# A hybrid attention and recurrence layer: the output-product units of one query tile put into other steps, and one unit moved forward from a later tile

## The chip, the cores and the metric

The kernel runs on one core of a Trainium2 chip. The metric is device time in microseconds, the median of the runs. The core has a matrix engine (PE, with its weight loads shown apart as PEld), a vector engine (DVE), a scalar engine (ACT), a general engine (POOL, also called GpSimd) and a queue engine (SP) that only issues transfers. Each works through its own instructions in the order in which the program wrote them, and waits at an instruction until what it needs is there.

## The reference

One encoder layer over 16 meta tokens and 1024 positions of width 1024:

```
u = rms_norm(h);  q, k, v, g_att, x_lru, g_lru = split(u @ w_in)
p1, p2 = softmax(q1 k1), softmax(q2 k2)      # four heads, two maps a head, chunk-causal
o = rms_norm((p1 - lam * p2) @ v) * silu(g_att)
y = rg_lru(conv(x_lru)) * silu(g_lru)        # a linear recurrence over the positions
h = h + concat(o, y) @ w_out;  return rms_norm(h)[meta tokens left out]
```

## The kernel before

The first part is the input projections, the recurrence and the gates. The rest, from about 245 us of the span, is the attention with the two output products; the change touches it. It works on eight tiles of 128 query rows, in the order 3, 7, 6, 5, 4, 2, 1, 0. Each tile has four **steps**, one for each head, so steps 4 to 7 are tile 7, steps 8 to 11 tile 6, 12 to 15 tile 5, 16 to 19 tile 4, 20 to 23 tile 2, 24 to 27 tile 1 and 28 to 31 tile 0. A tile sees only the keys up to its own end: its score rows are 784 wide in tile 5, 656 in tile 4, 400 in tile 2 and 272 in tile 1. Below, "(5,1,0)" is the first of the two maps of head 1 of tile 5.

A step runs work of four heads at different stages, in this order of writing (function `attend`):

- `transposes` of the head three steps back: PE turns the weights `w` into `pt`, and ACT copies `pt` to `wT`; for tiles 4 and up in two halves, one here and one later in the step;
- `scores`, first map: PE forms `pss`; DVE reads it with the mask, takes the extreme value `mx` and writes `e` (the custom instruction); ACT takes the exponential of `e` and its sum;
- **output-product units**, as many as one third of the step's number in the table `MF` asks for, rounded;
- `combine` of the head one step back: on DVE a reciprocal, a small product and one pass (`SCALAR_TENSOR_TENSOR`) that joins the two maps into `e`;
- units up to two thirds, then the second half of the transposes, `scores` of the second map, and the rest of the units;
- `halve`: DVE splits the joined weights into two 16-bit halves (`CAST` and `TENSOR_TENSOR`, both to `w`); POOL copies the first 16 columns (`wm`);
- `weighted` of the head four steps back: PE multiplies `wT` with the values into the bank `O`.

In the first steps the table places pieces of the value projection. From step 7 on a **unit** is half of an output product for 512 columns: six matmuls, `psol` for the recurrence part and `psoa` for the attention part. After each second unit the vector engine adds the bank to a row tile (`xres` or `res`). The units wait in a list `fill` and are taken in a fixed order; the table `MF` says only how many are written in which step. So the table decides what stands between two pieces of attention on PE, and, by the additions, on DVE.

When a tile's four heads are weighted, `finish` takes over, and its pieces are written between the units and steps as a planner's clock finds them due (`pace`, called after each unit, each `scores` and each `weighted`). The pieces: ACT copies the bank `O` to `o` and squares it head by head (`sq`, four instructions); DVE scales the sums (`sums`); POOL takes the power (`sums`, `pw`), multiplies (`rec`), and makes two passes over `o` (with `gate`, then with `rec`); PE transposes `o` into the bank `pa`; ACT copies it (`af`); POOL splits it into `at` (`CAST`, `TENSOR_TENSOR`). Tile 7 finishes in steps 12 to 14, tile 6 in 16 to 18, tile 5 in 20 to 23, tile 4 in 24 to 27.

Three PSUM banks serve `pt`, `ptm` (the transposed meta columns), `pa` and, up to step 19, `psol`; a bank taken by a `psol` whose two units stand in different steps is held over the steps between. Two double banks serve `pss`; from step 20 they are cut up: two single banks for `pss` and two for `psol` and `psoa`. Score rows therefore need the vector engine to have read the row two before. The recurrence part is loaded by POOL (`lr`) when the product before it starts.

Every engine instruction of this part goes through one helper, so the line shown is L77 throughout; groups are told apart by the names of their tiles.

Of the kernel before, what the change touches and what calls it, by code (L numbers as in the profile page):

```python
# [98 lines left out]
def hybrid_layer_kernel(ctx: ExitStack, tc: tile.TileContext, xT, x, meta, w6, nwT,  # L99
# [684 lines left out]
    def load_q(i):  # L784
        q = slot("work", [P, 2, NMAP, P], F16, name="qt")
        c = slice(i * P, (i + 1) * P)
        d = qk_d[G_Q]
        dma(q[:, 0], d[:, :, c].rearrange("m p t -> p m t"))
        dma(q[0:64, 1], d[:, 64:128, c].rearrange("m p t -> p m t"))
        dma(q[64:128, 1], d[:, 0:64, c].rearrange("m p t -> p m t"))  # L790
        QT[i] = q
# [112 lines left out]
    def combine(i, h):  # L904

        d = st[i]
        n = d["n"]
        e0, e1 = d["e"][h, 0], d["e"][h, 1]
        V.reciprocal(d["rec"][:, :, h], d["sm"][:, :, h])
        rat = d["mx"][:, 1, h:h + 1]  # L910
        V.tensor_scalar(rat, d["rec"][:, 1, h:h + 1], nlam, d["sm"][:, 0, h:h + 1], op0=OP.mult, op1=OP.mult)
        V.scalar_tensor_tensor(e0[:, 0:n], e1[:, 0:n], rat, e0[:, 0:n], op0=OP.mult, op1=OP.add)
        w = d["w"][h] = slot("work", [P, 2, T], F16, name="w16")
        if i in PH:
            A.copy(w[:, 0, 0:n], e0[:, 0:n])
# [218 lines left out]
    def pace():  # L1134
        if paced[0] is None:
            paced[0] = clock.now["PE"]
        while clock.now["PE"] - paced[0] >= CH:
            paced[0] += CH
            tick(CH)
# [11 lines left out]

    filled = [0]

    MF = [8, 5, 10, 5, 2, 5, 5, 4, 1, 3, 3, 0, 1, 1, 0, 2, 1, 2, 3, 0, 1, 2, 2, 0, 2, 3, 1, 2, 1, 3, 1, 3, 2, 3, 0, 0]

    def at_least(n):
        while fill and filled[0] < n:
            fill_one()
# [35 lines left out]
    def attend():  # L1194
# [4 lines left out]
        def trans(hl):  # L1199
            if tra:  # L1200
                i, h = tra
                if i < 4 and hl == 1:
                    return
                transposes(i, h, hl)
                pace()

        for s in range(NS + TL + 1):
# [10 lines left out]
            if cur:  # L1218
# [4 lines left out]
                if h == QH and i in after:  # L1223
                    load_q(after[i])
            at_least((MF[s] + 2) // 3)
            if com:
                combine(*com)
            at_least((2 * MF[s] + 2) // 3)
            trans(1)
            if cur:  # L1230
                scores(i, h, 1)
                pace()
            at_least(MF[s])
            if com:
# [101 lines left out]
```

## Time and profile before

| what | value |
|---|---|
| runs shown | 484.71, 485.53 and 485.62 us |
| median | 485.53 us |
| the profiled execution's own time | 484.72 us |
| its span, first to last instruction | 482.9 us |
| around the span | 1.8 us |
| granted TensorE clock, mean | 0.997 |

The busy shares of the span are 96% for PE, 76% for DVE, 63% for ACT and 26% for POOL. A row of the timeline gives the start, the length, the engine, the line, the operation with the tiles written and read, the shape and the count, and in brackets the idle time of that engine just before and what ended it. Consecutive instructions of one kind are one row, and the length of a matmul row includes its drain, so rows of PE overlap: distances of starts tell more than lengths. The chain of waits follows the end of the program back to what released each piece.

### The profile page before, as it was taken

Reading aid. Unit: us, or ns where it says so; the run is one execution under the profiler, and the core shown is the slowest. Engines: PE = TensorE matmul, PEld = TensorE weight load, DVE = VectorE, ACT = ScalarE, POOL = GpSimd, SP = SyncE. Lnnn points to the kernel's source line nnn. Section 1 sums busy time; section 2 is a strip of 40 time slices with the busy share of each in tenths; the row PEclk is TensorE's granted clock in tenths of the full one; section 3 lists DMA queues with packets and bytes.
Section 4 is the critical chain, followed back from the end, with each engine's and each line's share of the span. In section 5 each row is a group of like instructions: output and inputs, shape, how many; then the busy total and the mean of one; then the engine's idle time right before and its main releaser. Section 6 shows DMA issues by size and latency. Waiting matters only on the chain.

```text
span 482.9 us, 7747 instructions
## 1 busy us (share of the span) xinstructions
PE 464.7 (96%) x2844; PEld 375.5 (78%) x2844; DVE 365.6 (76%) x612; ACT 302.9 (63%) x591; POOL 125.8 (26%) x171
## 2 busy tenths in 40 slices
PE   6999999999999999999999999999988999999894
PEld 5998989988888888888876677777766778877783
DVE  5768987496798676974574476889999989898443
ACT  5788333673627838432583467698787877797633
POOL 0104102201110000000101054185142425365772
PEclk9999999999999999999999999999999999999998
DMA  7994321253022115249454134965943475405523
GB/s 225 385 393 163 103 73 46 66 154 88 23 69 85 44 43 175 87 149 331 135 163 163 45 77 141 257 166 101 263 111 99 132 186 153 126 28 198 195 88 131
DMA packets 50150, 68.33 MB, mean 141 GB/s; under 512 B 21008, under 2 KB 30128, under 8 KB 50112
## 3 DMA queue, kind: packets, MB, share of 16 engines
q1 hardware_dynamic: 38096, 55.00, 34.7%
q0 software_dynamic: 11872, 12.63, 11.4%
q8 instruction: 22, 0.36, 0.3%
q10 hardware_dynamic: 144, 0.20, 0.1%
q14 instruction: 16, 0.13, 0.1%
HBM read 48.91 MB, written 18.91 MB: 140 GB/s over the span
## 4 chain that ended last, share of the span: by engine, by line
PE 81%; DVE 10%; issue 3%; ACT 3%; DMA 1%; POOL 0%; POOLq 0%; DVEq 0%; ACTq 0%; SPq 0%
PE pss L77 39%; PE psv L77 9%; PE psol L77 7%; PE psoa L77 7%; PE psx L77 5%; PE O L77 4%; PE ps L77 3%; DVE e L77 3%; PE psg L77 2%; PE pt L77 2%; DVE w L77 2%; DVE sp L77 2%; DVE XL L77 1%; DVE xc L77 1%; PE psmr L77 1%
## 5 line engine op out<-in xcount | busy, mean ns | idle before, releaser
L77 PE MATMUL pss<-xs,w 128*128 128x512 f32 (+1 forms) x720 | 142.4, 345 | 4.2 <-ACT xs L77 4.2
L77 PEld LDWEIGHTS pss<-xs,w 128*128 128x128 f32 x720 | 120.4, 190 | 24.5 <-ACT xs L77 4.2
L77 ACT ACTIVATE e<-e,mx 128x528 f32<-128x528 f32 (+7 forms) x64 | 50.5, 789 | 27.4 <-DVE mx L77 26.1
L77 PE MATMUL psv<-w,xs 128*128 128x512 f32 x192 | 48.4, 403 | 0.2 <-DVE v L77 0.2
L77 DVE CUSTOM_DVE_ANT_0 e<-pss,mask,nesc 128x528 f32<-128x528 f32 (+6 forms) x56 | 42.6, 761 | 7.7 <-PE pss L77 6.5
L77 PE MATMUL pss<-w,xs 128*128 128x512 f32 x192 | 46.0, 394 | 0.0
L77 PE MATMUL psol<-woh,lr 128*128 128x512 f32 x128 | 42.8, 415 | 2.0 <-ACT wT L77 2.0
L77 DVE TENSOR_TENSOR w<-wraw,w 128x512 fp32r<-128x512 f32 (+2 forms) x49 | 31.7, 669 | 15.4 <-ACT w L77 15.3
L77 PE MATMUL pss<-kst,qt 128*128 128x512 f16 (+3 forms) x208 | 42.6, 318 | 0.7 <-DVE mx L77 0.7
L77 PEld LDWEIGHTS psv<-w,xs 128*128 128x128 f32 x192 | 35.3, 188 | 10.0 <-issue 0.8
L77 PEld LDWEIGHTS pss<-w,xs 128*128 128x128 f32 x192 | 35.7, 188 | 7.9
L77 PE MATMUL psoa<-woh,at 128*128 128x512 f32 (+1 forms) x136 | 41.6, 389 | 0.2 <-ACT psoa L77 0.2
L77 ACT COPY wT<-pt 128x1024 f16<-128x1024 f16 (+5 forms) x48 | 37.6, 784 | 1.0 <-PE pt L77 0.8
L77 DVE SCALAR_TENSOR_TENSOR e<-e,mx 128x528 f32<-128x528 f32 (+7 forms) x32 | 35.0, 1093 | 1.1
L77 ACT ACTIVATE w<-wraw 128x512 fp32r<-128x512 f32 x47 | 28.6, 621 | 10.4 <-DMA wraw<-in_w_dram 9.9
L77 PE MATMUL ps<-xs,w 128*128 128x512 f32 x120 | 34.4, 394 | 0.0
L77 PEld LDWEIGHTS <-wT 128*128 128x128 f16 x432 | 25.6, 98 | 6.6 <-issue 2.7
L77 PE MATMUL O<-v,wT 128*128 128x128 f16 x432 | 29.4, 219 | 1.3 <-ACT wT L77 1.3
L77 DVE TENSOR_TENSOR w<-e,w 128x528 f16<-128x528 f32 (+7 forms) x32 | 28.9, 904 | 0.9
L77 PEld LDWEIGHTS psol<-woh,lr 128*128 128x128 f32 x128 | 22.9, 188 | 8.6 <-ACT wT L77 3.2
L77 DVE RECIPROCAL a<-a 128x208 f32<-128x208 f32 x20 | 27.8, 1423 | 0.0
L77 PEld LDWEIGHTS psoa<-woh,at 128*128 128x128 f32 x136 | 24.1, 188 | 4.6 <-ACT psoa L77 0.4
(200 smaller groups left out, 838.3 us busy)
## 6 DMA issues: line engine op xcount, KB each, us to landing
wraw<-in_w_dram SPq DMA_DIRECT2D x47, 256.0 KB, 4.2
xt<-in_x_dram SPq DMA_DIRECT2D x8, 512.0 KB, 6.8
woraw<-in_w_out_dram SPq DMA_DIRECT2D x8, 512.0 KB, 3.5
xres<-in_x_dram SPq DMA_DIRECT2D x8, 512.0 KB, 4.6
lr<-lru_d POOLq DMA_DIRECT2D x8, 512.0 KB, 5.3
res_d<-xres SPq DMA_DIRECT2D x8, 512.0 KB, 3.2
res<-res_d SPq DMA_DIRECT2D x8, 512.0 KB, 4.4
out_dram<-res SPq DMA_DIRECT2D x7, 512.0 KB, 2.9
```

Of the source, the lines that this page charges most:

```text
L77: return f(*a, **k)
```

## The change

Five numbers of the table `MF` are changed. In steps 12 to 15 (tile 5) the units are 0, 2, 2, 1 where they were 1, 1, 0, 2: five in place of four. In step 21, the second step of tile 2, there is one in place of two. The sum over all steps is the same.

```
-    MF = [8, 5, 10, 5, 2, 5, 5, 4, 1, 3, 3, 0, 1, 1, 0, 2, 1, 2, 3, 0, 1, 2, 2, 0, 2, 3, 1, 2, 1, 3, 1, 3, 2, 3, 0, 0]
+    MF = [8, 5, 10, 5, 2, 5, 5, 4, 1, 3, 3, 0, 0, 2, 2, 1, 1, 2, 3, 0, 1, 1, 2, 0, 2, 3, 1, 2, 1, 3, 1, 3, 2, 3, 0, 0]
```

The instructions are the same, none is added or removed. Between step 14 and step 20 the program is one unit further on in the list than before, from step 21 on it is level again. The planner's clock also moves pieces of `finish`.

PE around the end of step 13 and step 14, before; `pa` is the transposed output of tile 7, `w_3324` the weights of head 3 of tile 6:

```order
L77 LDWEIGHTS wT
L77 MATMUL O<-v,wT 128x128
L77 MATMUL pa<-idf,o 128x128 x4
L77 LDWEIGHTS w_3324
L77 MATMUL pt<-idh,w_3324 128x128
```

and now, in step 14:

```order
L77 MATMUL pss<-kst,qt 128x272
L77 MATMUL psol<-woh,lr 128x512 x2
L77 MATMUL psol<-wol,lr 128x512
L77 MATMUL psol<-woh,lr 128x512 x2
L77 MATMUL psol<-wol,lr 128x512
L77 MATMUL pa<-idf,o 128x128 x4
L77 MATMUL psol<-woh,lr 128x512 x2
```

The transposition of tile 7's output stood directly behind step 13; it now has the first transposes and scores of step 14 and one unit ahead of it.

DVE in step 13, before; `sums_2521` are the sums of squares of tile 7:

```order
L77 ISA mx_3288 128x1
L77 TENSOR_SCALAR sums_2521<-sums_2521 128x4
L77 CAST w_3324<-e 128x912
L77 TENSOR_TENSOR w_3324<-e,w_3324 128x912
L77 ISA e,mx_3288<-pss,mask,nesc 128x784
L77 ISA mx_3288 128x1
L77 TENSOR_TENSOR xres<-xres,psol 128x512
```

and now:

```order
L77 ISA mx_3288 128x1
L77 CAST w_3307<-e 128x912
L77 TENSOR_TENSOR w_3307<-e,w_3307 128x912
L77 TENSOR_SCALAR sums_2521<-sums_2521 128x4
L77 ISA e,mx_3288<-pss,mask,nesc 128x784
L77 ISA mx_3288 128x1
```

The scaling of the sums has changed places with the two instructions that split the weights of head 3 of tile 6 (the number behind `w` is only that of the buffer).

DVE in steps 16 and 17, before; `sums_2918` are the sums of squares of tile 6, the 656-wide rows are the scores of tile 4:

```order
L77 RECIPROCAL rec_3289<-sums_3287 128x2
L77 TENSOR_SCALAR mx_3288<-rec_3289,nlam,sums_3287 128x1
L77 SCALAR_TENSOR_TENSOR e<-e,mx_3288 128x784
L77 ISA e,mx_3615<-pss,mask,nesc 128x656
L77 ISA mx_3615 128x1
L77 CAST w_3651<-e 128x784
L77 TENSOR_TENSOR w_3651<-e,w_3651 128x784
L77 TENSOR_SCALAR sums_2918<-sums_2918 128x4
```

and now:

```order
L77 TENSOR_TENSOR xres<-xres,psol 128x512
L77 RECIPROCAL rec_3289<-sums_3287 128x2
L77 TENSOR_SCALAR mx_3288<-rec_3289,nlam,sums_3287 128x1
L77 SCALAR_TENSOR_TENSOR e<-e,mx_3288 128x784
L77 TENSOR_SCALAR sums_2918<-sums_2918 128x4
L77 ISA e,mx_3627<-pss,mask,nesc 128x656
L77 ISA mx_3627 128x1
L77 CAST w_3658<-e 128x784
```

Here the scaling of the sums has moved forward, ahead of a row of scores and of the split, and an addition of a finished `psol` stands ahead of the reciprocal.

## The prediction

> **What bounds the kernel now.** I read the page's busy shares first, then the busy time by stretches of the span, then the chain of waits, then the timelines of PE and DVE from step 12 on.
>
> ```profile
> span 482.9 us, 7747 instructions
> PE 464.7 (96%) x2844; PEld 375.5 (78%) x2844; DVE 365.6 (76%) x612; ACT 302.9 (63%) x591; POOL 125.8 (26%) x171
> ...
> 363.00:378.00 15.00, 13.69 (x123) 10.18 (x120) 14.68 (x28) 12.39 (x29) 3.15 (x5) 1.00 0.56 141
> ...
> 393.00:409.00 16.00, 15.41 (x143) 12.68 (x143) 15.59 (x34) 13.45 (x36) 7.17 (x10) 1.00 0.61 149
> 409.00:425.00 16.00, 16.00 (x117) 12.93 (x116) 13.65 (x46) 12.34 (x37) 5.93 (x10) 1.00 0.39 116
> ```
>
> Over the whole span PE is the bound (96%), but the shares hide two stages. The columns of a stretch are its length, then PE, PEld, DVE, ACT and POOL. From 363 to 378 (tile 5 into tile 4) DVE is busy for 14.68 of 15.00 us and PE for 13.69. From 393 to 409 (tile 2) both are nearly full. From 409 on PE is full and DVE has room. The granted clock is 1.00 in all three. So DVE sets the pace in tile 5, the two run level in tile 2, and after that PE does. The chain says the same:
>
> ```profile
> 356.52 1.03 DVE e L77
> ...
> 371.12 0.94 DVE e L77
> ...
> 397.55 2.79 PE psol L77 x12
> ```
>
> It lies on DVE from 356.52 to 371.12 and on PE in tile 2. Where DVE leads, PE waits:
>
> ```profile
> 355.56 0.55 PE L77 MATMUL pt<-idh,w 128*128 128x128 f16 x7 [0.69 <-ACT wT L77]
> ...
> 359.43 0.66 PE L77 MATMUL pa<-idf,o 128*128 128x128 f32 x4 [1.49 <-POOL o L77]
> ...
> 365.89 0.73 PE L77 MATMUL psol<-woh,lr 128*128 128x512 f32 x2 [1.08 <-ACT wT L77]
> ...
> 378.39 0.73 PE L77 MATMUL psol<-woh,lr 128*128 128x512 f32 x2 [0.30 <-ACT wT L77]
> ...
> 393.59 0.50 PE L77 MATMUL pss<-kst,qt 128*128 128x400 f16 x2 [0.67 <-DVE mx L77]
> ```
>
> That is 3.56 us before tile 2 and 0.67 at its first scores. There both PE and DVE meet: the banks of `pss` are cut up at that point, so PE may not go on before DVE has read the last row of tile 4. This wait makes the sum simple. Up to it only the time at which DVE arrives counts, and PE's work ahead of it is free as long as it fits into the 4.23 us of waits. Behind it PE has the work that is left.
>
> **The change part by part.** *The unit.* The chain's row gives 2.79 us for twelve matmuls, so a unit of six is 1.40 us of PE. One more stands ahead of the meeting point, one fewer behind it. If DVE arrives at the same time and never holds PE up afterwards, the program ends 1.40 us earlier: **−1.40**. PE's waits have room for it, 4.23 against 1.40. The addition to `xres` after each second unit moves along, but both orders have five of them ahead of tile 2's first row of scores; the sixth follows it at once now, and one step later before.
>
> *DVE up to the meeting point.* It has four gaps or coming gaps:
>
> ```profile
> 354.75 0.17 DVE L77 TENSOR_SCALAR sums<-sums 128x4 f32<-128x4 f32 x1 [0.85 <-ACT sq L77]
> ...
> 387.06 0.90 DVE L77 CUSTOM_DVE_ANT_0 e<-pss,mask,nesc 128x656 f32<-128x656 f32 x1 [0.55 <-PE pss L77]
> ...
> 388.49 0.69 DVE L77 TENSOR_TENSOR xres<-xres,psol 128x512 f32<-128x512 f32 x1 [0.52 <-PE psol L77]
> ...
> 416.14 0.17 DVE L77 TENSOR_SCALAR sums<-sums 128x4 f32<-128x4 f32 x1 [1.89 <-ACT sq L77]
> ```
>
> The first goes: the scaling of tile 7's sums now stands behind a `CAST` and a `TENSOR_TENSOR`. ACT's squares also start one `wT` copy later, so I look at whether the cover is enough:
>
> ```profile
> 354.62 0.88 ACT L77 COPY wT<-pt 128x896 f16<-128x896 f16 x1
> 355.41 0.95 ACT L77 ACTIVATE e<-e,mx 128x784 f32<-128x784 f32 x1
> ```
>
> A copy takes 0.79 from start to start, so the squares end at about 355.5. DVE is free 0.85 ahead of 354.75, at 353.9; it first spends on the two what lies today between the scaling (354.75) and the next row of scores (356.52 in the chain), 1.7 us, and reaches the scaling at about 355.6. So **−0.85**; without that cover it would be the 0.79 again.
>
> The scaling of tile 6's sums moves the other way, ahead of a row of scores:
>
> ```profile
> 370.44 0.68 DVE L77 TENSOR_TENSOR xres<-xres,psol 128x512 f32<-128x512 f32 x1
> ...
> 374.81 1.03 DVE L77 SCALAR_TENSOR_TENSOR e<-e,mx 128x784 f32<-128x784 f32 x1
> ...
> 377.56 0.78 ACT L77 COPY wT<-pt 128x768 f16<-128x768 f16 x1
> ```
>
> DVE ends the joining pass at 375.84; ACT's next instruction behind the four squares starts at 377.56. In today's times DVE would stand for 1.7 us, less the 0.6 (0.68 with its overlap) of the addition that now lies ahead: **+1.1**. Bounds: 0 if ACT's squares come earlier than DVE does, 1.89 as in the row of tile 4's sums, which has this very order. Behind DVE then wait ACT's exponentials and PE's second scores of step 16.
>
> The two gaps at 387.06 and 388.49 are PE's: it came late with scores and a unit. PE now has one unit done already, so these go, −1.07. Something takes their place. The third unit of step 18 now needs the bank of `pa`, so it waits for ACT's copy `af`, and with it PE's scores of the last head of tile 4. The nearest price is a wait for the same kind of copy, 1.08 in the list above; bounds 0 and 1.49. I take **0** for these two together. The wait for `pa` itself (1.49) shrinks, since a unit and a row of scores now cover it; PE's waits there cost nothing while DVE leads.
>
> *Collisions of DVE and POOL.* The same pass takes very different times:
>
> ```profile
> 398.61 0.17 DVE L77 TENSOR_SCALAR sums<-sums 128x4 f32<-128x4 f32 x1
> ...
> 400.35 2.37 DVE L77 SCALAR_TENSOR_TENSOR e<-e,mx 128x400 f32<-128x400 f32 x1
> ...
> 406.02 0.64 DVE L77 SCALAR_TENSOR_TENSOR e<-e,mx 128x400 f32<-128x400 f32 x1
> ...
> 407.59 1.53 DVE L77 TENSOR_TENSOR w<-e,w 128x400 f16<-128x400 f32 x1
> ...
> 411.60 0.57 DVE L77 TENSOR_TENSOR w<-e,w 128x400 f16<-128x400 f32 x1
> ```
>
> ```profile
> 401.00 1.27 POOL L77 TENSOR_TENSOR o<-o,gate 128x512 f32<-128x512 f32 x1
> ...
> 407.41 1.27 POOL L77 TENSOR_TENSOR at<-af,at 128x512 fp32r<-128x512 f32 x1
> ```
>
> Where one of POOL's passes runs, DVE's pass is 1.73 (2.37 less 0.64) or 0.96 (1.53 less 0.57) longer. The number of passes is unchanged, only who meets whom. In tiles 5 and 4 I put **+0.2** for one more small hit, with bounds of −0.96 and +1.73.
>
> The Trainium skill ("SBUF — State Buffer", section "Who interferes with whom") says that a DVE instruction with two SBUF inputs and a GpSimd instruction that reads SBUF lock each other out, and the first holds the ports for its whole length. By it one hit costs at most one POOL pass, 1.27; the 1.73 here is more, so the trace agrees with the kind of the effect but not with that bound. With 1.27 as the upper bound this term would end 0.46 lower.
>
> *Up to the meeting point:* −0.85 + 1.1 + 0 + 0.2 = **+0.45**: DVE is a little later there.
>
> *Behind it.* With a unit less in step 21, PE comes sooner to scores whose banks DVE must have read:
>
> ```profile
> 409.72 0.39 PE L77 MATMUL pss<-kst,qt 128*128 128x272 f16 x2
> ```
>
> ```profile
> 409.04 0.62 DVE L77 CUSTOM_DVE_ANT_0 e<-pss,mask,nesc 128x400 f32<-128x400 f32 x1
> ```
>
> The first scores of tile 1 use the bank that DVE has read by 409.66, 0.06 ahead of them. So 1.34 of the 1.40 would come back as a wait if DVE stayed where it is. It does not: with the addition gone from between the sums (398.61) and the joining pass (400.35), the pass starts 0.60 sooner after the sums, 1.14 in place of 1.74 behind them; at 0.64 it is over at 1.78, before POOL's pass, 2.39 behind the sums, begins. That saves 1.73, and about 1.0 of it comes back, because POOL then meets the split that follows. The pair that POOL writes to `at` has moved behind tile 2's last head, which saves the 0.96. So DVE gains 1.7 there, less the 0.45 from before: 1.25 of the 1.34 needed. I add **+0.1**, and **+0.15** for the transposition of tile 5's output, which now stands between transposes and scores of step 23 with no unit to cover it. Bounds 0 and 1.40.
>
> Behind tile 2 the wait of 1.89 for tile 4's sums leaves DVE, but PE is full there and gains nothing.
>
> *Sum:* −1.40 + 0.45 + 0.25 = **−0.70 us**. The profiled execution took 484.72 us, 482.9 of span and 1.8 around it; the sum gives 484.0 for it, 482.2 of span. The median of the runs, 485.53, is 0.8 above that execution, so I forecast **484.8 us**.
>
> **The rivals.** *A: all of it counts, and more.* Tile 6's squares are ready when DVE comes (0 for 1.1), as DVE has been held by a collision or an addition, and DVE keeps pace in tile 2. Then −1.40 − 0.85 = −2.25: 483.3 us. For it: every PE wait above has room. Against: ACT is busy for 12.39 of 15.00 us there.
>
> *B: DVE is the clock to the end of tile 2.* The moved scaling costs the whole 1.89 of its nearest row, which less 0.85 makes DVE 1.04 late at the meeting point, and DVE stays level in tile 2, so the unit taken from step 21 returns as a wait: 486.6 us, slower. It decides as soon as DVE is late by more than it gains from POOL's shifted passes. For it: 15.59 of 16.00 us. Against: those passes must hit as before.
>
> *C: the waits only change places.* DVE arrives as before, and 1.34 return in front of tile 1's scores: 485.5 us.
>
> A late load is a smaller risk. POOL now issues the next `lr` behind the power of tile 7's sums, so at about 357 and a half, and the product that needs it comes at about 366. The longest way to landing in the row below would make that product about 1 us late, in a stage in which PE waits anyway.
>
> ```profile
> DMA to landing us min/median/max: 4.5/5.3/9.4
> ```
>
> **How the numbers follow.** A change of 0.2%, 0.97 us, is about what a measurement of this kernel can tell from none. The forecast has a chance of 0.46, with 484.1 to 485.6 as its own range; I put 0.16 of it to faster and 0.30 to the same. A has 0.22, all faster. B has 0.20, of which 0.19 is slower and 0.01 the same. C has 0.12: 0.11 the same, 0.01 slower. Together 0.38 faster, 0.42 the same, 0.20 slower. The range reaches to A and to B: 483.1 to 486.6 us.
>
> **What would show it.** Right: DVE's 0.85 before tile 7's sums is gone, and about 1.1 stands before tile 6's sums; PE's wait at tile 2's first scores is shorter than today's and ends 0 to 0.9 us later than 393.59; one unit fewer follows it; the joining pass behind tile 5's sums takes about 0.64 instead of 2.37; PE reaches tile 1's first scores at about 409.0. Wrong: the pass is still above 2 us, or PE idles for over 1 us in steps 21 to 24 (then B or C); PE is let through to tile 2's first scores before 393.0 (then A). A tail behind 436 us that moves by itself would break the sum, since I took it as unchanged.

## The result and the profile after

The changed kernel takes 488.17 us (median of 5 runs, 487.72 to 488.64) against 485.31 (5 runs of the kernel before beside it): a ratio of 1.0057, 95% interval 1.0046 to 1.0067. It is 2.9 us slower; the forecast was 484.8, 0.7 faster.

The page of the changed kernel, its span and busy shares:

```profile
span 486.9 us, 7751 instructions
PE 465.3 (96%) x2844; PEld 375.6 (77%) x2844; DVE 368.4 (76%) x612; ACT 302.8 (62%) x591; POOL 126.0 (26%) x171
```

PE's busy time grew by 0.6 us, DVE's by 2.8. The span grew by 4.0, but the profiled execution is already 0.96 us late at the first score row of tile 5 on DVE (351.27 against 350.31), where the programs are still the same; 3.0 remain. From here on times are compared between marks on DVE: its first score row of tile 5, of tile 2, of tile 1 and of tile 0. Busy time between these marks, of the kernel before (columns as in the prediction):

```profile
350.31:394.74 44.43, 39.96 (x386) 30.97 (x384) 41.66 (x80) 35.75 (x79) 15.88 (x23) 1.00 0.52 137
394.74:412.09 17.35, 17.35 (x158) 14.12 (x157) 16.87 (x40) 13.81 (x39) 7.38 (x11) 1.00 0.50 123
412.09:427.81 15.72, 15.72 (x123) 12.69 (x122) 13.41 (x42) 12.86 (x39) 7.98 (x11) 1.00 0.39 117
```

and of the changed one:

```profile
351.27:397.70 46.43, 41.91 (x389) 32.52 (x389) 43.92 (x80) 35.76 (x79) 16.57 (x23) 1.00 0.51 131
397.70:415.16 17.46, 16.13 (x152) 13.04 (x151) 16.91 (x40) 14.54 (x40) 7.40 (x11) 1.00 0.51 136
415.16:430.38 15.22, 15.22 (x120) 12.06 (x119) 13.92 (x43) 11.61 (x37) 6.48 (x11) 1.00 0.34 107
```

Tiles 5 and 4 (the first row) take 2.00 us more, and DVE's busy time in them grows by 2.26 over the same 80 instructions. Tile 2 takes as long as before with one unit of PE fewer: PE has 1.33 us of room there that it lacked. Tile 1 takes 0.50 less. The rest, to PE's last matmul, is 1.37 longer (50.02 against 48.65). Together +2.98.

Which of DVE's instructions grew is seen in its groups by shape between the first two marks (busy time, mean ns of one, idle time before). Before:

```profile
L77 DVE CUSTOM_DVE_ANT_0 e<-pss,mask,nesc 128x784 f32<-128x784 f32 x8 | 8.2, 1027 | 0.0
...
L77 DVE SCALAR_TENSOR_TENSOR e<-e,mx 128x784 f32<-128x784 f32 x4 | 5.3, 1333 | 0.1
...
L77 DVE SCALAR_TENSOR_TENSOR e<-e,mx 128x656 f32<-128x656 f32 x3 | 3.4, 1123 | 0.1
...
L77 DVE CAST w<-e 128x784 f16<-128x784 f32 x4 | 2.2, 562 | 0.0
...
L77 DVE CAST w<-e 128x656 f16<-128x656 f32 x3 | 1.6, 534 | 0.0
```

After:

```profile
L77 DVE CUSTOM_DVE_ANT_0 e<-pss,mask,nesc 128x784 f32<-128x784 f32 x8 | 8.2, 1027 | 0.0
...
L77 DVE SCALAR_TENSOR_TENSOR e<-e,mx 128x784 f32<-128x784 f32 x4 | 6.1, 1520 | 0.1
...
L77 DVE CAST w<-e 128x784 f16<-128x784 f32 x4 | 3.2, 802 | 0.0
L77 DVE SCALAR_TENSOR_TENSOR e<-e,mx 128x656 f32<-128x656 f32 x3 | 2.9, 973 | 0.1
...
L77 DVE CAST w<-e 128x656 f16<-128x656 f32 x3 | 2.6, 871 | 0.0
```

The custom rows are the same to the nanosecond. The joining passes of 784 columns grew by 4 × 0.19, the copies by 4 × 0.24 and 3 × 0.34, and the joining passes of 656 columns shrank by 3 × 0.15: +2.3 in all. The single ones, in DVE's timeline of the changed kernel (start, duration, operation, wait before):

```profile
356.51 0.17 DVE L77 TENSOR_SCALAR sums<-sums 128x4 f32<-128x4 f32 x1
...
358.05 2.97 DVE L77 SCALAR_TENSOR_TENSOR e<-e,mx 128x784 f32<-128x784 f32 x1
...
367.94 1.52 DVE L77 CAST w<-e 128x784 f16<-128x784 f32 x1
...
379.51 0.17 DVE L77 TENSOR_SCALAR sums<-sums 128x4 f32<-128x4 f32 x1 [1.30 <-ACT sq L77]
...
390.57 1.63 DVE L77 CAST w<-e 128x656 f16<-128x656 f32 x1
...
404.48 1.75 DVE L77 CAST w<-e 128x400 f16<-128x400 f32 x1
406.26 1.30 DVE L77 TENSOR_TENSOR w<-e,w 128x400 f16<-128x400 f32 x1
...
413.69 1.54 DVE L77 TENSOR_TENSOR w<-e,w 128x400 f16<-128x400 f32 x1
```

and what POOL does beside the long ones:

```profile
357.78 0.94 POOL L1045 DMA_DIRECT2D lr<-lru_d  x1
...
358.90 1.28 POOL L77 TENSOR_TENSOR o<-o,gate 128x512 f32<-128x512 f32 x1
...
367.75 1.29 POOL L77 TENSOR_TENSOR at<-af,at 128x512 fp32r<-128x512 f32 x1
...
390.55 1.28 POOL L77 TENSOR_TENSOR at<-af,at 128x512 fp32r<-128x512 f32 x1
...
404.69 1.30 POOL L77 TENSOR_TENSOR o<-o,gate 128x512 f32<-128x512 f32 x1
406.07 1.05 POOL L77 TENSOR_TENSOR o<-o,rec 128x512 f32<-128x512 f32 x1
...
413.38 1.43 POOL L77 TENSOR_TENSOR at<-af,at 128x512 fp32r<-128x512 f32 x1
```

Each long pass lies on a pass of POOL over 128x512. I call what a pass takes beyond its usual time (1.03 for a joining pass of 784 columns, 0.90 of 656, 0.64 of 400; 0.56, 0.50 and 0.36 for the copies; 0.57 for the second half of the split of 400) its **held time**; differences of up to 0.12 us are not counted. Now 4.25 us are held between the first two marks (1.94, 0.96 and 1.13 in the rows above, and 0.22 in a joining pass at 383.27). Before, it was 1.86, in three joining passes, which lay on passes of POOL too:

```profile
358.58 1.62 DVE L77 SCALAR_TENSOR_TENSOR e<-e,mx 128x784 f32<-128x784 f32 x1
...
364.03 1.64 DVE L77 SCALAR_TENSOR_TENSOR e<-e,mx 128x784 f32<-128x784 f32 x1
...
380.07 1.56 DVE L77 SCALAR_TENSOR_TENSOR e<-e,mx 128x656 f32<-128x656 f32 x1
```

```profile
356.99 1.27 POOL L77 TENSOR_TENSOR o<-o,gate 128x512 f32<-128x512 f32 x1
358.34 1.04 POOL L77 TENSOR_TENSOR o<-o,rec 128x512 f32<-128x512 f32 x1
...
363.57 1.27 POOL L77 TENSOR_TENSOR at<-af,at 128x512 fp32r<-128x512 f32 x1
...
379.67 1.27 POOL L77 TENSOR_TENSOR o<-o,gate 128x512 f32<-128x512 f32 x1
```

DVE's waits there went from 1.92 to 1.66.

PE shows DVE's lateness as waits. In step 23 it stands for 1.33 in front of `pa`, about the length of the unit that it no longer has in step 21; the last row is a wait in the tail that the kernel before does not have:

```profile
361.67 0.74 PE L77 MATMUL psol<-woh,lr 128*128 128x512 f32 x2 [1.74 <-DVE xres L77]
...
396.55 0.50 PE L77 MATMUL pss<-kst,qt 128*128 128x400 f16 x2 [0.59 <-DVE mx L77]
...
409.92 0.63 PE L77 MATMUL pa<-idf,o 128*128 128x128 f32 x4 [1.33 <-ACT wT L77]
...
412.66 0.40 PE L77 MATMUL pss<-kst,qt 128*128 128x272 f16 x2
...
449.60 0.33 PE L77 MATMUL O<-v,wT 128*128 128x128 f16 x3 [0.71 <-ACT o L77]
```

The chain of waits names the held passes too; "issue" at 358.19 is the long joining pass, which waits for nothing that the profile shows:

```profile
358.19 2.76 issue
...
368.03 1.45 DVE w L77
...
404.56 1.68 DVE w L77
```

### The profile page after: what moved, and what is told of

It is laid out like the page before. It is cut to its first block, busy times and chain, and to the rows that moved or that the text cites. A ratio compares the mean times of both kernels' runs of the same rounds, so it can differ in the third digit from the quotient of the medians.

```text
span 486.9 us, 7751 instructions
## 1 busy us (share of the span) xinstructions
PE 465.3 (96%) x2844; PEld 375.6 (77%) x2844; DVE 368.4 (76%) x612; ACT 302.8 (62%) x591; POOL 126.0 (26%) x171
## 4 chain that ended last, share of the span: by engine, by line
PE 70%; DVE 15%; issue 5%; ACT 4%; DMA 4%; SPq 1%; POOL 0%; POOLq 0%; DVEq 0%; ACTq 0%
PE pss L77 35%; PE psv L77 9%; PE psoa L77 7%; PE psol L77 5%; DVE e L77 5%; DVE w L77 4%; PE ps L77 3%; PE O L77 3%; PE psg L77 2%; PE psx L77 2%; DMA xt<-in_x_dram 2%; DVE sp L77 2%; PE pt L77 2%; DMA wraw<-in_w_dram 1%; DMA xraw<-in_xT_dram 1%
## 5 line engine op out<-in xcount | busy, mean ns | idle before, releaser
L77 DVE TENSOR_TENSOR w<-wraw,w 128x512 fp32r<-128x512 f32 (+2 forms) x49 | 31.7, 670 | 14.8 <-ACT w L77 14.7
L77 DVE TENSOR_TENSOR w<-e,w 128x528 f16<-128x528 f32 (+7 forms) x32 | 30.0, 936 | 0.9
```

What stands on the lines that cost most here:

```text
L77: return f(*a, **k)
```

## The experiments

Theory 1 came from this comparison: up to tile 1 DVE is the clock, and it is late because more of its passes meet POOL's; the 0.9 behind that come from ACT's order at the end. The rivals, called theory 2 in the expectations, were waits (tile 6's sums, banks) or PE's time for the units. The table gives, for each kernel, the median, its ratio to the kernel before in the same session (95% interval; "one run" where there was no timing), and from its profile the two stretches of DVE, from tile 5's to tile 2's first row and on to tile 1's, each as length (held, waits).

| kernel | us | ratio | tiles 5 and 4 | tile 2 |
|---|---|---|---|---|
| before | 485.31 | | 44.43 (1.86, 1.92) | 17.35 (2.97, 0) |
| changed | 488.17 | 1.0057 [1.0046, 1.0067] | 46.43 (4.25, 1.66) | 17.46 (3.07, 0) |
| only steps 12–15 | 498.10 | 1.0252 [1.0228, 1.0276] | 46.42 (4.23, 1.67) | 17.45 (2.46, 0) |
| only step 21 | 489.78 | 1.0094 [1.0078, 1.0111] | 44.45 (1.89, 1.95) | 14.80 (0.48, 0) |
| changed, no passes over `o` | 484.45 | 0.9986 [0.9977, 0.9995] | 44.28 (2.07, 1.67) | 15.71 (0.93, 0.31) |
| before, no passes over `o` | 484.11 | 0.9974 [0.9962, 0.9987] | 43.78 (0.61, 2.43) | 17.06 (0.96, 1.44) |
| changed, tile 6's sums on POOL | 487.61 | 1.0047 [1.0035, 1.0060] | 45.65 (4.78, 0.48) | 17.48 (3.07, 0) |
| changed, `o` copied first | 487.38 | 1.0040 [1.0028, 1.0053] | 46.42 (4.23, 1.67) | 17.46 (3.07, 0) |
| before, unit from 21 to 24 | 488.94 | 1.0078 [1.0065, 1.0090] | 44.47 (1.90, 1.93) | 14.81 (0.48, 0) |
| before, sums 7 and 4 on POOL | 484.73 | 0.9988 [0.9978, 0.9998] | 43.42 (1.65, 1.31) | 17.36 (2.98, 0) |
| changed, no gate pass of tile 7 | 486.13 | one run | 44.50 (2.27, 1.69) | 17.45 (3.06, 0) |
| changed, no `rec` pass of tile 7 | 487.88 | one run | 46.44 (4.22, 1.69) | 17.46 (3.06, 0) |
| before, unit from 21 to 20 | 486.06 | 1.0009 [1.0001, 1.0017] | 44.46 (1.89, 1.93) | 18.12 (3.05, 0.62) |
| the same, sums 7 and 4 on POOL | 485.49 | 1.0001 [0.9991, 1.0012] | 44.38 (1.13, 2.02) | 18.13 (3.06, 0.62) |
| changed, passes swapped | 484.58 | 0.9985 [0.9976, 0.9994] | 45.32 (3.02, 1.68) | 15.84 (1.44, 0) |
| before, passes swapped | 484.49 | 0.9985 [0.9976, 0.9993] | 44.70 (2.37, 1.79) | 17.05 (2.39, 0) |
| before, swapped, sums 7 and 4 on POOL | 483.59 | 0.9971 [0.9962, 0.9981] | 43.50 (1.64, 1.31) | 17.05 (2.36, 0) |
| changed, all three undone | 483.57 | 0.9971 [0.9960, 0.9981] | 44.69 (3.80, 0.50) | 15.83 (1.43, 0) |

The first length less held time and waits is 40.4 to 40.8, whether four or five units stand in it (41.2 in the one row with unit and sums moved, whose profiled execution, 486.52, is 1.0 above that kernel's median); the second is 14.3 to 14.7, and 15.0 where one addition to `xres` more falls into it (only steps 12–15). So DVE's own work is fixed, and its held time and waits account for each length to about 0.3. PE's units enter only where DVE waits for them. As DVE is either busy or idle, this sum says where the time lies; what causes the held time is shown by the edits below.

**The two halves of the change.**

```
-  MF[12:16] = 1, 1, 0, 2        (the other half: -  MF[21] = 2)
+  MF[12:16] = 0, 2, 2, 1                         +  MF[21] = 1
```

> Only the four numbers of steps 12 to 15 are changed; the second step of tile 2 keeps its two products. Theory 1 (DVE sets the pace to the end of tile 2, and hits of its passes by POOL's passes make it late; the product taken out of the second step of tile 2 gained nothing): tile 2's first scores come about 2.0 us later than before, counted from the start of step 12, as in the changed kernel, tile 1's first scores also about 2.0 (up to 2.3) later, and the whole is 487.3 to 488.2, depending on the order at the end. Theory 2 (DVE's collisions matter little, the waits on PE count, and a product fewer is worth its 1.40 us): tile 1's first scores come 3.4 us later than before, and the whole is 488.7 or more.

> Only the second step of tile 2 is changed, from two products to one. Up to tile 2's first scores nothing differs from before. Theory 1 (DVE sets the pace there): the product's 1.40 us come back as waits before tile 1's first scores, which come 0 to 0.3 us earlier than before; the whole is 485.0 to 485.6, plus what another order at the end costs. Theory 2 (PE sets the pace): tile 1's first scores come 1.2 to 1.4 earlier, and the whole is 483.9 to 484.1.

The first half reaches tile 2 1.99 and tile 1 2.09 later than before, as theory 1 said, and equal to the changed kernel with its unit fewer: in that company the unit in step 21 is worth nothing on DVE's clock. That the two lengths of tile 2 agree is in part chance: with the unit, one addition more (about 0.6) stands there, and 0.61 less is held. The second half gave neither theory's number: tile 1's first row came 2.53 us earlier (+0.02 in the first stretch, −2.55 in the second), more than the unit's 1.40. DVE's timeline and POOL's of that kernel show why:

```profile
404.15 1.12 DVE L77 SCALAR_TENSOR_TENSOR e<-e,mx 128x400 f32<-128x400 f32 x1
```

```profile
403.56 1.28 POOL L77 TENSOR_TENSOR o<-o,gate 128x512 f32<-128x512 f32 x1
```

Only 0.48 is held in tile 2, where before had 2.97: the 2.49 of difference are the gain. Both whole times were missed by far, on the other side of tile 1. Either half alone changes the count, so every later unit stands one place from where it stood, beside other pieces of `finish`; that this is the reason is not shown. PE's timeline of the first half has a wait of 3.18 for DVE at tile 0's last scores and later ones for ACT and POOL; the rest of the program is 6.8 us longer than before (55.45 against 48.65), and 6.9 in the second half (55.54):

```profile
448.87 0.29 PE L77 MATMUL pss<-kst,qt 128*128 128x144 f16 x2 [3.18 <-DVE mx L77]
...
480.86 0.49 PE L77 MATMUL psoa<-woh,at 128*128 128x512 f32 x1 [1.39 <-POOL at L77]
```

What each of these end waits hangs on was not followed up.

**POOL's two passes left out for tiles 7, 6 and 5.**

```
-  G.tensor_tensor(o, o, g); G.tensor_tensor(o, o, rec)
+  if i in (7, 6, 5): clock.step("G", ...) twice      # the planner's clock only
```

> The changed kernel with POOL's two passes over o (by the gate and by rec, 1.3 to 1.7 us each) left out for tiles 7, 6 and 5, everything else in the same order. Theory 1 (hits by these passes make DVE late): DVE's joining pass at 358.05 falls from 2.97 to about 1.04, the copy at 367.94 or 390.57 may still be held, as it meets the passes of the projection's operand, which stay; tile 2's first scores come 1.5 to 2.2 earlier than in the changed kernel, and the whole is 486.0 to 486.8. Theory 2 (the waits for tile 6's sums and for the banks of PE cause the loss): tile 2's first scores move by less than 0.5, and the whole is 487.7 to 488.2.

> The kernel before with the same two passes over o left out for tiles 7, 6 and 5. In its trace three passes of DVE are held there, by 1.84 us together, most of them beside these passes. Theory 1: it is 0.5 to 1.5 us faster than before, 483.8 to 484.8, and the run of the changed kernel without these passes lies only 1.0 to 1.9 above it (tile 6's sums and the end), where the two kernels lie 2.9 apart. Theory 2: the distance stays at 2.5 to 3.0.

The joining pass fell from 2.97 to 1.03 and tile 2's first row came 2.15 earlier. The two kernels, 2.9 apart, now lie 0.34 apart, less than theory 1 had asked for, and the changed one lies below its range, because tile 2 lost 1.75 as well. In the kernel before the gain is smaller, as waits for PE take the place of held time (1.92 to 2.43, and 0 to 1.44). By these two profiles the changed kernel is still 0.50 longer up to tile 2 and 1.22 behind tile 0's first row, and 1.63 shorter in between. The waits of theory 2 cannot be the main loss: DVE's 1.30 for tile 6's sums is still there, and so is PE's of 1.26 for ACT's copy `wT` (at 384.88 in the changed kernel, at 382.40 here).

**Tile 6's sums, and ACT's order at the end.**

```
+  if i == 6: nc.gpsimd.tensor_scalar(so, so, 1/P, eps)   else: V.tensor_scalar(...)
```

> The changed kernel with the scaling of tile 6's sums done by POOL instead of DVE, all else in the same order. Theory 1 (DVE's own line of held passes and waits is the clock): the wait of 1.30 at 379.51 leaves DVE and tile 2's first scores come earlier by it, less or more by what new meetings with POOL cost (each up to 1); the whole is 486.2 to 487.6. Rival (the wait has PE or ACT beside it that is as late): tile 2's first scores move by less than 0.3, and the whole is 487.9 to 488.4.

The wait of 1.30 left DVE, and 0.53 of it went into new held time (a copy of 1.27 at 383.46 in place of 0.50, a joining pass no longer held by 0.22): 0.78 earlier at tile 2, 0.56 in the median, just above the range.

```
   if h == NH - 1:                  # in weigh, for tile 1
+      f = finish(i); next(f); chain(f)      # copy O to o at once
```

> The changed kernel with ACT's copy of tile 1's O put back ahead of the wT copy and the square, where it stood before the change. Theory 1 (this order costs the last 0.9): PE's wait of 0.71 at 449.60 goes, the distance to before falls by 0.7 to 0.9 from there to the end, and the whole is 487.2 to 487.5. Rival (the end is set by the later wait for a wT copy, which takes up what is won): 488.0 to 488.3.

As theory 1 said: 0.79 back, and the rest of the program is 49.18 instead of 50.02. The change had moved ACT's copy of tile 1's `O` behind a `wT` copy and a square, and PE may not write the next `O` before it.

**The unit of step 21 with the count kept.**

```
-  MF[20:25] = 1, 2, 2, 0, 2
+  MF[20:25] = 1, 1, 2, 0, 3        (then: 2, 1, 2, 0, 2)
```

> The kernel before with one product moved out of tile 2's second step (two to one) into tile 1's first (two to three), so that the count is kept and later products stand where they stood. Theory 1 (what counts is which of DVE's passes meet POOL's): as in the run of that step alone, the joining pass that took 2.37 before and the pass that took 1.53 fall to about 0.6 to 1.1; tile 1's first scores come 2.0 to 2.6 earlier, and the whole is 483.0 to 484.4, with up to 0.9 lost again at the end, where ACT's copy of tile 1's O stands one place later. Theory 2 (the products' time on PE counts): 1.4 earlier at tile 1's first scores, given back in its first step, and the whole is 485.0 to 485.5.

> The kernel before with one product moved from tile 2's second step (two to one) into its first (one to two); the order behind these steps is that of before, the tail too. Theory 1 (DVE's held passes and waits decide, the place of the product does not): tile 1's first scores move by the change in DVE's held time and waits between tile 2's first scores and these, to within 0.2, and the whole by the same; POOL's order there is nearly that of before, so the pair of passes meets about the same passes: 484.6 to 485.9. Theory 2 (PE sets the pace): 1.4 later in the first step and 1.4 back in the second, 485.0 to 485.5, with tile 2's second scores 1.2 to 1.4 later.

The first repeats the gain in tile 2 (−2.54, held 0.48) and loses it again: 2.17 in tile 1, where PE is full, and 4.2 at the end, where PE waits for ACT, among others here. Its 488.94 is far above both ranges, so a count that is kept does not keep the tail:

```profile
473.80 0.70 PE L77 MATMUL psoa<-woh,at 128*128 128x512 f32 x2 [1.45 <-ACT psoa L77]
```

The second keeps the end and the meetings, and tile 2 grows by 0.77, of which 0.62 are new waits of DVE (ACT's squares, `psol`) and 0.08 held: the sum holds, but the place of the unit is not free, as theory 1 had it. Its whole time, 486.06, is just above theory 1's range.

**The sums of tiles 7 and 4 on POOL.**

> The kernel before with the scaling of tile 7's and of tile 4's sums done by POOL instead of DVE, all else in the same order. DVE's waits for them (0.85 at 354.75 and 1.89 at 416.14) leave it. Theory 1 (held passes and waits of DVE add up): tile 2's first scores come 0.85 earlier less what changes in meetings with POOL, which also moves (in the changed kernel the same wait went and a pass was held 1.9 longer): -1.0 to +1.5; what is won behind 416 is kept to the end of tile 1 at most; the whole is 483.0 to 486.5. Theory 2 (PE sets the pace): 485.0 to 485.5.

> The same move of one product between tile 2's first two steps, and the scaling of tile 7's and tile 4's sums done by POOL. If what each brings adds up: 0.5 below the run of the move alone, as the scaling by itself was 0.5 below before; 484.0 to 485.4. If the meetings with POOL fall anew: up to 1.5 to either side of that.

On the kernel before it gains 0.5 in the median (up to tile 2 held time is 0.21 and waits are 0.61 less); on the version with the moved unit it is 0.57, which ends just above its range. The profile of that version is of a longer execution and does not show the gain. The edit is the one above, for tiles 7 and 4.

**Which of POOL's passes holds.**

```
-  G.tensor_tensor(o, o, g)         (the other: -  G.tensor_tensor(o, o, rec))
+  if i == 7: clock.step(...)        else: as before
```

> The changed kernel with only tile 7's pass of o by the gate left out on POOL (its pass by rec stays). It asks what holds DVE's joining pass at 358.05 for 1.94 longer than its 1.03. If one pass of POOL holds it at a time: the pass by rec now starts where the gate's did, meets the joining pass in the same way, and it is held 0.9 to 1.3 (2.0 to 2.4 in all); tile 2's first scores come 0.6 to 1.0 earlier than in the changed kernel. If only the gate's pass held it: it falls to 1.03, and they come 1.5 to 1.9 earlier.

> The changed kernel with only tile 7's pass of o by rec left out on POOL (its pass by the gate stays). If the joining pass at 358.05 is held over both passes of POOL, which follow one another within 0.1: it is held about 1.3 instead of 1.94 (2.3 in all). If the gate's pass alone holds it: it stays at 2.97.

Without the gate's pass the joining pass takes its 1.03; without the pass by `rec` it is as long as ever (DVE's and POOL's timelines of that kernel):

```profile
357.29 2.96 DVE L77 SCALAR_TENSOR_TENSOR e<-e,mx 128x784 f32<-128x784 f32 x1
```

```profile
358.14 1.27 POOL L77 TENSOR_TENSOR o<-o,gate 128x512 f32<-128x512 f32 x1
```

So one pass holds, for 1.93, longer than its own row. Where the gate's pass is left out, the pass by `rec` moves up, but it begins at 358.66, behind the joining pass (357.49 and 1.03 long), and meets only the addition and a custom row, which it does not hold. The issue of the load `lr` (357.22, 0.94) lies on the joining pass there too, so it alone does not hold it. One edit of one tile gives back 1.93 at tile 2.

**The same two passes in the other order.** Nothing is left out, and the planner's clock is told the old order, so that every other instruction keeps its place.

```
-  G.tensor_tensor(o, o, g); G.tensor_tensor(o, o, rec)
+  G.tensor_tensor(o, o, rec); G.tensor_tensor(o, o, g)
```

> The changed kernel with POOL's two passes over o in the other order for every tile: first by rec, then by the gate, so that the gate's pass starts about 1.1 later. If the place of the gate's pass decides: tile 7's joining pass of 2.97 falls to 1.0 to 1.1; the gate's pass then runs beside the next custom pass, and may hold the copy or the product of w after it by up to 1; tile 2's first scores come 0.9 to 1.9 earlier than in the changed kernel, and the whole is 486.0 to 487.6. If what counts is that there are two passes: no change, 487.8 to 488.5.

> The kernel before with the same two passes in the other order. If the place of the gate's pass decides: the joining pass held by 1.73 at 400.35 and the one held by 0.66 at 380.07 get free, others may be met anew; tile 1's first scores move by the sum of DVE's held times to within 0.3; 484.0 to 486.0 for the whole. If two passes as such count: 485.0 to 485.6, and the same passes held.

> The kernel before with the two passes in the other order and the scaling of tile 7's and tile 4's sums on POOL. If both gains add: 0.5 below the run with the other order alone; if the meetings fall anew, up to 1 to either side of that: 483.3 to 486.0.

> The changed kernel with all three undone at once: POOL's two passes in the other order, tile 6's sums scaled on POOL, and ACT's copy of tile 1's O ahead of the wT copy and the square. If the losses are separate, the gains add: 484.58 less 0.8 for the copy, less 0.6 for the sums: 483.2, in a range of 482.7 to 483.7. If the sums on POOL only move the passes into other meetings: 483.7 to 484.6.

On the changed kernel it takes 3.6 us off, more than expected. In tile 7's finish the gate's pass has moved off the joining pass, behind a custom row, onto a copy that takes 1.50 instead of 0.56:

```profile
357.54 1.03 DVE L77 SCALAR_TENSOR_TENSOR e<-e,mx 128x784 f32<-128x784 f32 x1
...
360.04 1.50 DVE L77 CAST w<-e 128x784 f16<-128x784 f32 x1
```

```profile
358.71 1.04 POOL L993 TENSOR_TENSOR o<-o,rec 128x512 f32<-128x512 f32 x1
359.83 1.28 POOL L994 TENSOR_TENSOR o<-o,gate 128x512 f32<-128x512 f32 x1
```

Tiles 5 and 4 gain 1.11 and tile 2 gains 1.62, which I had not foreseen (held 3.07 to 1.44). So the loss hangs on where the pass falls, not on how much POOL does.

On the kernel before the joining pass at 400.35 gets free, as expected, but not the one at 380.07 (still held, by 0.56), and other passes are met. Tile 1's first row comes only 0.03 earlier; of the 0.6 that the median gains, 0.56 lie behind tile 0's first row in the profile, where they were not followed. The gains add roughly: with the sums of tiles 7 and 4 on POOL the kernel before comes to 483.59, 1.5 below its own reference where the two edits alone gave 0.6 and 0.5. The changed kernel with all three losses undone comes to 483.57, where the sum of the gains gave 483.2. Both beat before and changed alike.

## Why the prediction was wrong

*The unit, −1.40.* Failed. Up to tile 1 it moved DVE's clock by nothing (17.46 with one product in step 21, 17.45 with two); PE shows it as the wait of 1.33. Tile 1 is 0.50 shorter, but that this is the unit's is not shown. That PE "has the work that is left" behind the meeting point was wrong: DVE leads to the end of tile 2, where it never waits and PE is busy for 16.13 of 17.46.

*Tile 7's sums, −0.85.* Right: no wait at 356.51.

*Tile 6's sums, +1.1.* Right in kind, 1.30 measured, 0.78 of it on the clock, since without the wait another pass is met.

*The gaps at 387.06 and 388.49, 0.* Better than said: of 1.07, 0.36 is left. The bank of `af` cost 0.56 on PE at 389.84 and 0.36 on DVE. The waits up to tile 2 make −0.26 where I had +0.25.

*Collisions in tiles 5 and 4, +0.2.* This is the step that failed. It measured +2.39 (1.86 to 4.25), beyond its own bound of +1.73. I bounded it by one hit more, as if the number of meetings were a small error around today's. But a stall that goes shifts DVE against POOL for a whole `finish`. The gate's pass of tile 7 started 0.47 into a custom row before (356.99 against 356.52), and now 0.85 into the joining pass (358.90 against 358.05), which is held by 1.94. Both engines moved: counted from tile 5's first row, the joining pass comes 1.49 earlier (6.78 for 8.27), as the wait of 0.85 is gone and an addition now follows it, and the gate's pass 0.95 later (7.63 for 6.68). I had seen that POOL's load of `lr` moved behind the power of tile 7's sums and asked only whether the load comes late; its issue takes POOL 0.94 ahead of the gate's pass. That the place of this pass decides is shown by the edits; how much of the shift is the load's and how much DVE's was not tested. The passes at 367.94 and 390.57, on POOL's split of `af`, add 0.96 and 1.13; no edit took these two away.

*Behind the meeting point, +0.25.* Failed by the same step. The joining pass behind tile 5's sums took 0.64, as forecast, but the split behind it was held for 2.11 where I put 1.0, and the 0.96 that I took as saved came back at 413.69. DVE gained nothing in tile 2 (17.46 for 17.35) in place of 1.7, so the unit came back as a wait. Without the first half of the change the same edit took 2.55 off tile 2: the term hangs on where POOL's passes lie.

*The tail, 0.* It cost 0.87 net of tile 1, by ACT's order, and the run with that copy put back returned 0.79. I had taken it as unchanged because the list of units is level again from step 21; but the planner places the pieces of `finish` by its clock.

*The sum:* +2.00 up to tile 2 (−0.26 waits, +2.39 held, −0.13 overlaps), +0.11 in tile 2 and +0.87 behind, 2.98 of span, 2.86 in the medians, against −0.70.

*The rivals.* B had the mechanism (DVE the clock to the end of tile 2, the unit back as a wait) and the sign, but its price came from the sums (1.04) and not from the passes, so its 486.6 is 1.6 short. A and C fell. Of the signs listed, the wait before tile 6's sums and the pass of 0.64 came as said. PE was let through to tile 2's first scores 2.0 us later than before (396.55 less the late start, against 393.59), where the sign asked for 0 to 0.9; it reached tile 1's first scores at 412.66, or 411.7 without the late start, where the forecast had 409.0, and idled for 1.33 in step 23, the sign named for B or C.

## What to carry to other kernels

Where a vector engine that sets the pace shares time with POOL, a forecast needs a list of which pass lies beside which: length = fixed work + held time + waits held here to about 0.3 us in seventeen of eighteen profiles. Removing a stall on one engine moves all later meetings, so its gain is not safe until these are laid out again. A cheap lever is the order of POOL's own passes: with the same work it gave 3.6 us on the changed kernel and 0.6 on the kernel before, there not by fewer holds up to tile 1. And units that move change the later program, too: half of a balanced edit cost 4.6 and 12.9 us, and one that kept its total still lost 4.2 at the end.

## What was not expected of the hardware

One pass of POOL of 1.27 held one pass of DVE by 1.93 (2.96 for 1.03), with the pass that followed it left out. The Trainium skill ("SBUF — State Buffer", section "Who interferes with whom") lets the first of two such instructions hold the ports for its own length; the trace agrees that there is a hold but shows a longer one, on a pass that by its row had begun 0.85 ahead of POOL's (357.29 against 358.14), though POOL's spans are rough.

The sizes follow a pattern. In 103 of the 106 held passes of the eighteen profiles, between tile 5's and tile 1's first rows, the held pass ends a fixed time behind the end of a pass of POOL: 0.82 to 0.84 for a joining pass of 784 columns, 0.69 to 0.71 of 656 and 0.41 to 0.45 of 400, 0.42 to 0.43, 0.35 to 0.37 and 0.21 to 0.24 for the copies, and 0.42 to 0.44 for the second half of the split of 400. Each is 0.1 to 0.2 less than the pass takes alone, as if nearly all of it ran behind POOL's. So the hold is the time from DVE's start to the end of POOL's pass, less 0.1 to 0.2: 0.85 + 1.28 − 0.19 = 1.94 at 358.05, and 0.65 + 1.27 − 0.19 = 1.73 at 400.35 in the kernel before. The other three, copies held by 0.14 to 0.23, lie on POOL's issue of the load `lr`.

Which of the two is held stays open; the starts in the rows do not decide it. In the changed kernel the copy at 404.48 was held by 1.39, though the gate's pass began 0.21 behind it. In the one with the passes swapped the second half of a split (403.27) took its usual 0.58, and the pass by `rec`, begun 0.10 behind it, took 1.38, where its shortest is 1.04.

What was never held is as plain: the custom rows, which read a bank of PSUM, took 1.03 (x8) in both kernels, and the additions of a bank to `xres` 0.68, beside whatever POOL did, as the same section says of an instruction with at most one SBUF input outside the two-port modes.
